# Transposes of small expert steps on 80 rows, and products that shift low parts upward on all 128 partitions

## The chip, the cores and the metric

The kernel runs on one core of a Trainium2 chip. The metric is the device time of one execution in microseconds (us). The kernel before took 1118.21 us, the median of 3 runs (1115.34 to 1118.33).

## The reference

One layer of a streaming encoder over 1024 tokens of width 1024, all in float32: a norm, one input projection, two mixers side by side (a spatial gating unit and a chunked linear recurrence), an output projection with a residual, and then a hierarchical mixture of experts with a residual and a last norm. The change touches the experts alone. Each token goes to one of 4 groups and to 2 of the 8 experts in that group:

```python
h = jax.nn.silu(xb @ w_gate[e]) * (xb @ w_up[e])
return h @ w_down[e]
```

`xb` holds the tokens of expert `e` (rows of 1024), `w_gate` and `w_up` are 1024x512 for each of the 32 experts, `w_down` is 512x1024. The results are weighted and added to the tokens' rows.

## The kernel before, in words

**Stages.** The mixers, the output projection and the router come first. From about 480 us on the kernel works through 32 expert steps; what follows is about those. The steps take the experts in the order of their number of tokens. The host code fixes a capacity for each place: 96 rows for the first three, then two places of 192 rows (a block of 128 and one of 64), and then single blocks of 128, 96, 80 and, for the 18 last, 64 rows. `KINDS` (line 51) mixes them: "s" is a small step of 64 rows, "L" a larger one of 80 to 128, "B" one of two blocks. So there are 20 blocks of 64 rows (18 of "s", and the second of each "B"), and nine times an "L" stands between small steps or after one, most often as s L s L.

**Precision.** Every float32 operand is taken apart into a high part (rounded to the matmul's format) and a low part (what is left), since TensorE reads the high format. Weights: `esplit` makes `ehi` on ScalarE (line 198) and `elo` on VectorE (line 199), a tile of 128x1024 at a time, from a raw tile `eraw` that a DMA brought. There are four buffers of `ehi` and of `elo`; raw tiles lie in a ring of 14 buffers of 1 MB, and at most four loads are in flight (`raw`, line 1030 on).

**Blocks over 64 rows** use three products for each piece of weights (`mm3`, lines 258 to 260): high by high, high by low, low by high, with the tokens as the stationary operand.

**Blocks of 64 rows** pack both parts of the tokens in one stationary operand of 128 columns: columns 0 to 63 the high part, 64 to 127 the low part (`split_rows`, `parts`, `block_mm`, lines 1059 and 1060). Two products do, and the sum stands in PSUM in two halves: partitions 0 to 63 hold the high part's, 64 to 127 the low part's. The halves have to be added. `low_out` (line 1096) copies partitions 64 to 127 from PSUM to a tile `low` on ScalarE (lines 1102, 1105); `low_in` (line 1108) then adds them into partitions 0 to 63 by a product of `low` with an identity `low_id` that stands on partitions 64 to 127 (line 1111): 64 contracted rows, 64 columns out, a moving operand of 512 columns. There is one such product for the gate sum and one for the up sum, and two for the down sum (`pair`, 1024 wide).

**Transposes.** The gathered tokens `xg` are turned by TensorE against `ident` (`xT`, line 1005: two groups of four transposes for a block), and so is the hidden activation `hh` (`hT_`, line 1022: one group of four). A transpose of a block of m rows contracts m rows and moves m columns. ScalarE and VectorE split what comes out into `x` and `h`. `hh` is written by a Silu on ScalarE (line 1119) and a multiplication on VectorE (line 1122), on m partitions.

**Order.** The code writes the order of every engine out by hand: `units` lists, quarter by quarter, the gate (G), up (U) and down (D) products of the steps, and `more` hangs the rest behind quarters. The low product of G stands behind the second quarter of U, and directly behind it the next step's first group of token transposes; the low product of U stands behind the second quarter of the D that follows. In most of the kernel D runs one step late.

Of the kernel before, what the change touches and what calls it, by code (L numbers as in the profile page):

```python
# [9 lines left out]
F32R = mybir.dt.float32r  # L10
BF16 = mybir.dt.bfloat16
I32 = mybir.dt.int32
AF = mybir.ActivationFunctionType
# [5 lines left out]
P = 128  # L19
# [33 lines left out]
HALF = 64  # L53
# [4 lines left out]
ORDER = (10, 0, 6, 7, 9, 1, 2, 3, 4, 5, 11, 12, 13, 8)  # L58
NXG = 5
AHEAD = 3  # L60
EPS = 1e-6


# [5 lines left out]
def body(ctx, tc, x, norm1_gain, w_in, v_gain, w_s, b_s, lower, out_gain, w_out, norm2_gain,  # L69
         w_gr, b_gr, w_er, b_er, w_gate, w_up, w_down, final_gain, out):  # L70
    nc = tc.nc
    V, A, T, G = nc.vector, nc.scalar, nc.tensor, nc.gpsimd
# [8 lines left out]
    def capacity(n):  # L81
        return STEP0 if n < FIXED else LEAST + MORE * sum(n < bound for bound in BOUNDS)
# [10 lines left out]
    def const(shape, dt, name):  # L93
        return consts.tile(shape, dt, name=name)

    ident = const([P, P], F32, "ident")
    V.memset(ident, 1.0)
    G.affine_select(ident, ident, pattern=[[1, P]], compare_op=OP.is_equal, fill=0.0, base=0, channel_multiplier=-1)

    low_id = const([P, HALF], F32R, "low_id")  # L100
    A.copy(low_id[HALF:], ident[HALF:, HALF:])
    before = const([P, P], BF16, "before")
    V.memset(before, 1.0)
    G.affine_select(before, before, pattern=[[1, P]], compare_op=OP.is_gt, fill=0.0, base=0, channel_multiplier=-1)
# [8 lines left out]
    eps = const([P, 1], F32, "eps")  # L113
    V.memset(eps, EPS)
    down8 = const([P, EPG], F32, "down8")
# [43 lines left out]
    def tp():  # L159
        return tpp.tile([P, 4, P], F32, name="tp", bufs=2)  # L160
# [34 lines left out]
    def split(hi, lo, raw, gain=None, sub=V):  # L195

        if gain is None:
            A.copy(hi, raw)  # L198
            sub.tensor_tensor(lo, raw, hi.bitcast(F32), op=OP.subtract)  # L199
        else:  # L200
            A.mul(hi, raw, gain)
            V.scalar_tensor_tensor(lo, raw, gain, hi.bitcast(F32), op0=OP.mult, op1=OP.subtract)  # L202
# [28 lines left out]
    def rstd(ss, n, pool, name, w):  # L231
        r = pool.tile([P, w], F32, name=name)
        A.activation(r, ss, AF.Sqrt, bias=eps, scale=1.0 / n)
        V.reciprocal(r, r)
        return r
# [13 lines left out]
    def norm_back(t):  # L249
        for half in range(2):  # L250
            pt = tp()
            for k in range(4):
                T.transpose(pt[:, k, :], n1s[t][:, (4 * half + k) * P:(4 * half + k + 1) * P], ident)
            hi = nh[:, 4 * half:4 * half + 4, t * P:(t + 1) * P]
            split(hi, nl[:, 4 * half:4 * half + 4, t * P:(t + 1) * P], pt)
# [17 lines left out]
    def proj_n(chunk, t, between=None):  # L273
        acc = bank("acc", 4)[:, :256]
        for k in range(KT):
            hi, lo = chunk["N"][k]
            ts = slice(P * t, P * t + P)
            mm3(acc, k, KT, nh[:, k, ts], nl[:, k, ts], hi, lo)
            if between and k == KT // 2 - 1:
                between()  # L280
        return acc
# [51 lines left out]
    for t in range(NT):  # L333
        if 1 < t < NT - 1:
            norm_back(t + 1)
        acc = proj_n(chunks[0], t, (lambda: norm_back(t + 1)) if t < 2 else None)
# [44 lines left out]
    while n < NE:  # L381
        c, o = capacity(n), n
# [150 lines left out]
    for p in range(2):  # L533
# [6 lines left out]
        for t in range(NT):  # L540
            acc = proj_n(chunk, t)
# [7 lines left out]
        r = rstd(ss, P, gp, "rsv", NT * 2)  # L549
# [7 lines left out]
        for half in range(2):  # L557
            for g in range(2):
# [4 lines left out]
                m = gp.tile([P, 4, P], F32, name="m", bufs=4)  # L563
# [7 lines left out]
        for g in range(2):  # L571
            gg = 2 * p + g
            accs = proj_t(chunk, g)
            if gg == H - 1:
# [3 lines left out]
                for k, (tag, n) in zip((4, 6, 0, 2), (("ht", 4), ("n2", 2), ("hT", 1), ("n2", 2))):  # L578
                    r = ra.tile([P, 2, 512], F32, name="woraw", tag=tag, bufs=n)
# [188 lines left out]
    def last_stats(half):  # L768

        t = NT - 1  # L770
        if half == 0:
# [3 lines left out]
            gained(t, 0)  # L775
            late[HOLD[0]] = V.tensor_scalar(rr[t][:, 0:1], rr[t][:, 0:1], 1.0 / D, EPS, op0=OP.mult, op1=OP.add)
            return
# [8 lines left out]
    def gained(t, half):  # L786
        cs = slice(512 * half, 512 * half + 512)
        G.tensor_tensor(n2s[t][:, cs], hts[t][:, cs], g2[:, cs], op=OP.mult)
# [23 lines left out]
    for k in (4, 6, 0, 2):  # L812
        r = wo1[k]
# [46 lines left out]
    low, high = range(4), range(4, KT)  # L860
# [45 lines left out]
    def open_pool(name, side="left"):  # L906
        return est.enter_context(tc.tile_pool(name=name, bufs=1, side=side, reuse_waits="tile"))
# [7 lines left out]
    es = open_pool("es")  # L915
# [48 lines left out]
        st["sl"].append((sl, m))  # L964

    fin = {}

    def next_xg():
        while any(xgs[nblk[0] % NXG] is v for v in fin.values()):
            nblk[0] += 1  # L970
        xg = xgs[nblk[0] % NXG]
        nblk[0] += 1
        return xg
# [12 lines left out]
    def split_rows(name, k, bufs, m):  # L986
        if m > HALF:
            return [ep.tile([P, k, P], F32R, name=name, bufs=bufs) for _ in range(2)]
        return [ep.tile([P, k, P], F32R, name=name, bufs=bufs)]

    def parts(tiles, ks, m):

        if m > HALF:
            return [t[:, ks, :m] for t in tiles]
        return [tiles[0][:, ks, c:c + m] for c in (0, HALF)]

    def xT(st, b, half, pts=None):

        (sl, m), xg = st["sl"][b], st["xg"][b]
        if half == 0:  # L1000
            st["x"].append(split_rows("x4", KT, 4, m))
        xv = xg.rearrange("p (c k) -> p k c", k=KT)
        pt = pts[half] if pts else tp()
        for k in range(0 if pts else 4):
            T.transpose(pt[:, k, :m], xv[:m, 4 * half + k, :], ident[:m, :m])  # L1005
        if half == 0 and st["plain"] == PLAIN0:

            st["xf"] = es.tile([P, 2 * 512], F32, name="xf0", tag="low")[:, :4 * m].rearrange("p (k c) -> p k c", k=4)
            V.tensor_copy(st["xf"], pt[:, :, :m])
        elif half == 1 and st["plain"] == PLAIN1:  # L1010
            st["xf"] = xfp.tile([P, 4, HALF], F32, name="xf")
            V.tensor_copy(st["xf"][:, :, :m], pt[:, :, :m])
            return
        split(*parts(st["x"][b], slice(4 * half, 4 * half + 4), m), pt[:, :, :m])

    def hT_(st, b):
        (sl, m), hh = st["sl"][b], st["h"][b]
        hv = hh.rearrange("p (c k) -> p k c", k=4)
        tiles = split_rows("h4", 4, 3, m)
        pt = tp()  # L1020
        for k in range(4):
            T.transpose(pt[:, k, :m], hv[:m, k, :], ident[:m, :m])
        split(*parts(tiles, slice(0, 4), m), pt[:, :, :m])
        st["hT"].append(tiles)

# [65 lines left out]
    def scatter(dst, sl, m, y, **how):  # L1091
        nc.gpsimd.indirect_dma_start(  # L1092
            out=dst[:, :], out_offset=bass.IndirectOffsetOnAxis(ap=sl[:m, 0:1], axis=0),
            in_=y[:m], in_offset=None, bounds_check=S - 1, oob_is_err=False, **how)

    def low_out(st, which):

        for acc, (sl, m) in zip(st["acc"][which], st["sl"]):
            if m <= HALF:
                low = es.tile([P, 2, 512], F32R, name="low", tag="low")  # L1100
                if which == 2:
                    A.copy(low[HALF:], st["pair"][HALF:])
                for c, a in enumerate(acc):
                    if which < 2:
                        A.copy(low[HALF:, c], a[HALF:])
                    st["low"].append((a[:m], low_id[HALF:, :m], low[HALF:, c]))

    def low_in(st):

# [4 lines left out]
    def post(st, which, last=False):  # L1114
        for b, (sl, m) in enumerate(st["sl"]):
            acc = st["acc"][which][b]
            if which == 0:
                st["h"].append(ep.tile([P, FE], F32, name="hh", bufs=2))
                A.activation(st["h"][b][:m], acc[0][:m], AF.Silu)
            elif which == 1:  # L1120
                hh = st["h"][b]
                V.scalar_tensor_tensor(hh[:m], acc[0][:m], sl.bitcast(F32)[:m, 2:3], hh[:m], op0=OP.mult, op1=OP.mult)
            else:
                y = yp.tile([P, D], F32, name="y", bufs=2)
                if b == len(st["sl"]) - 1:
                    A.copy(y[:m].rearrange("p (c n) -> p c n", c=2), st["pair"][:m])  # L1126
                else:
                    for c in range(2):
                        A.copy(y[:m, c * 512:(c + 1) * 512], acc[c][:m])
                st["y"].append(y)  # L1130
                if not last:
                    scatter(h_d, sl, m, y, compute_op=OP.add)
# [38 lines left out]
    def new_step(e, plain=()):  # L1171
        return dict(e=e, sl=[], xg=[], x=[], h=[], hT=[], y=[], low=[], acc={}, plain=plain)
# [121 lines left out]
    def prepare(s_):  # L1294

        while started[0] <= min(s_ + 1, NE - 1):
            start_step(started[0])
            started[0] += 1
        while listed_[0] <= min(s_ + 1, NE - 1):
            list_step(listed_[0])  # L1300
            listed_[0] += 1
        while gathered[0] <= min(s_, NE - 1):
            gather(sts[gathered[0]])
            gathered[0] += 1
# [80 lines left out]
    sts[0]["xg"].append(xgs[0])  # L1385
    prepare(AHEAD - 1)
    for half in range(2):
        xT(sts[0], 0, half, x0)
    i = 0
    for u in units:  # L1390
# [14 lines left out]
        else:  # L1405
# [3 lines left out]
            if which == 0 and q == 0:  # L1409
                prepare(s_ + AHEAD)  # L1410
                if NE // 2 <= s_ < NE // 2 + 5:
# [5 lines left out]
    st = sts[last]  # L1417
# [10 lines left out]
    with tc.For_i(0, n_ov, 1) as j:  # L1428
# [3 lines left out]
        st = new_step(e)  # L1432
# [45 lines left out]
```

## Time and profile before

| | |
|---|---|
| median of 3 runs | 1118.21 us |
| profiled execution, whole | 1115.45 us |
| its span, first to last instruction | 1113.5 us |
| share of the span: TensorE (PE), VectorE (DVE), ScalarE (ACT), GpSimd (POOL) | 95%, 73%, 68%, 17% |
| DMA, mean over the span | 238 GB/s |

PE is busy nearly all the time, but its records overlap: a product's record lasts from its start until its result has left the array, so what a product costs in a row of products is the distance from its start to the next start. The prediction reads PE by such distances.

### The profile page before, as it was taken

What the parts mean: (1) busy time and instruction counts of PE and PEld (TensorE: products, weight loads), DVE (VectorE), ACT (ScalarE), POOL (GpSimd) and SP (SyncE); (2) the same over time, 40 slices, a digit from 0 to 9 for tenths busy, and PEclk for the clock granted to TensorE, in tenths of its full rate; (3) what the DMA queues carried; (4) which work ended last, traced back from release to release, by engine and by line L of the source; (5) the groups of instructions that cost most, each with busy time, mean ns of one, the idle gap of its engine ahead of it and who ended that gap; (6) DMA issues with size and microseconds to landing.
All of it is one profiled execution on the core that took longest, in us unless ns stands there. A gap on an engine that the chain in (4) does not pass through costs nothing.

```text
span 1113.5 us, 16412 instructions
## 1 busy us (share of the span) xinstructions
PE 1061.1 (95%) x5602; PEld 816.0 (73%) x5602; DVE 809.9 (73%) x1438; ACT 758.4 (68%) x1058; POOL 188.8 (17%) x203
## 2 busy tenths in 40 slices
PE   7999999999999999998999999999999999999962
PEld 7978989899898898776667667667666666666531
DVE  6576665664544555757996799998879999999773
ACT  7665564654323432546887898998889889998783
POOL 3000000000002121543112222312213212121022
PEclk9999999999999999868999999999999999999986
DMA  8211111111115351599998999999999999999943
GB/s 272 87 39 39 39 39 39 38 39 33 45 39 178 106 215 46 213 401 340 380 393 315 325 373 377 400 366 368 361 322 384 382 371 388 381 386 394 353 145 100
DMA packets 67797, 264.75 MB, mean 238 GB/s; under 512 B 9990, under 2 KB 32574, under 8 KB 42112
## 3 DMA queue, kind: packets, MB, share of 16 engines
q1 hardware_dynamic: 54896, 230.72, 55.0%
q0 software_dynamic: 12528, 31.92, 10.3%
q8 instruction: 45, 0.74, 0.3%
q10 hardware_dynamic: 288, 1.05, 0.2%
q14 instruction: 40, 0.33, 0.1%
HBM read 244.60 MB, written 24.81 MB: 242 GB/s over the span
## 4 chain that ended last, share of the span: by engine, by line
PE 26%; DMA 11%; ACT 9%; DVE 4%; issue 3%; POOL 0%; POOLq 0%; ACTq 0%; SPq 0%; DVEq 0%
ACT ehi L198 5%; DMA eraw<-in_w_down_dram 5%; PE acc L258 4%; PE acc L259 3%; PE acc L260 3%; DMA eraw<-in_w_up_dram 3%; DVE elo L199 3%; PE acc L1060 2%; DMA eraw<-in_w_gate_dram 2%; PE acc L1059 2%; PE tp L1005 2%; PE pair L258 1%; PE pair L259 1%; PE pair L260 1%; PE pair L1060 1%
## 5 line engine op out<-in xcount | busy, mean ns | idle before, releaser
L199 DVE TENSOR_TENSOR elo<-eraw,ehi 128x1024 fp32r<-128x1024 f32 x374 | 442.6, 1218 | 64.1 <-ACT ehi L198 61.5
L198 ACT CAST ehi<-eraw 128x1024 fp32r<-128x1024 f32 x374 | 379.8, 1050 | 30.5 <-PE acc L260 8.8
L1060 PE MATMUL acc<-elo,x 128*128 128x512 f32 x304 | 124.5, 410 | 9.3 <-DVE elo L199 8.8
L1092 POOL DMA_INDIRECT h_d<-y,sl x34 | 57.5, 1693 | 425.6 <-ACT y L1126 367.4
L1059 PE MATMUL acc<-ehi,x 128*128 128x512 f32 x304 | 125.6, 413 | 2.5 <-ACT ehi L198 2.4
L258 PE MATMUL acc<-whiN,nh 128*128 128x256 f32 x384 | 109.0, 284 | 1.8 <-ACT nh L198 1.8
L260 PE MATMUL acc<-whiN,nl 128*128 128x256 f32 x384 | 108.3, 282 | 0.6 <-DVE nl L199 0.6
L259 PE MATMUL acc<-wloN,nh 128*128 128x256 f32 x384 | 108.4, 282 | 0.1
L258 PE MATMUL acc<-ehi,x 128*96 128x512 f32 (+2 forms) x220 | 89.6, 407 | 0.0
L259 PE MATMUL acc<-elo,x 128*96 128x512 f32 (+2 forms) x220 | 87.1, 396 | 0.0
L260 PE MATMUL acc<-ehi,x 128*96 128x512 f32 (+2 forms) x220 | 86.7, 394 | 0.0
L1060 PEld LDWEIGHTS acc<-elo,x 128*128 128x128 f32 x304 | 57.4, 189 | 33.9 <-DVE elo L199 23.4
L259 PE MATMUL acc<-nl,whiT 128*128 128x512 f32 x192 | 77.7, 405 | 0.0
L258 PE MATMUL acc<-nh,whiT 128*128 128x512 f32 x192 | 77.5, 404 | 0.0
L260 PE MATMUL acc<-nh,wloT 128*128 128x512 f32 x192 | 77.0, 401 | 0.0
L258 PEld LDWEIGHTS acc<-whiN,nh 128*128 128x128 f32 x384 | 72.4, 188 | 2.2 <-ACT nh L198 2.1
L260 PEld LDWEIGHTS acc<-whiN,nl 128*128 128x128 f32 x384 | 72.3, 188 | 0.8 <-DVE nl L199 0.8
L1059 PEld LDWEIGHTS acc<-ehi,x 128*128 128x128 f32 x304 | 58.1, 191 | 20.0 <-issue 6.2
L259 PEld LDWEIGHTS acc<-wloN,nh 128*128 128x128 f32 x384 | 72.3, 188 | 0.5 <-DVE wloN L202 0.3
L1059 PE MATMUL pair<-ehi,h 128*128 128x512 f32 x160 | 67.5, 422 | 0.9 <-DVE h L199 0.9
L1060 PE MATMUL pair<-elo,h 128*128 128x512 f32 x160 | 65.1, 407 | 0.9 <-DVE elo L199 0.7
L580 POOL DMA_DIRECT2D woraw<-in_w_out_dram x4 | 2.8, 717 | 325.1 <-PE acc L260 325.1
(382 smaller groups left out, 2182.1 us busy)
## 6 DMA issues: line engine op xcount, KB each, us to landing
eraw<-in_w_gate_dram SPq DMA_DIRECT2D x64, 1024.0 KB, 10.3
eraw<-in_w_up_dram SPq DMA_DIRECT2D x64, 1024.0 KB, 11.2
eraw<-in_w_down_dram SPq DMA_DIRECT2D x64, 1024.0 KB, 10.6
wraw<-in_w_in_dram SPq DMA_DIRECT2D x96, 128.0 KB, 2.4
ht<-in_x_dram SPq DMA_DIRECT2D x8, 512.0 KB, 3.8
eraw<-h_d SPq DMA_DIRECT2D x4, 1024.0 KB, 7.8
out_dram<-eraw SPq DMA_DIRECT2D x4, 1024.0 KB, 4.2
h_d<-ht POOLq DMA_DIRECT2D x7, 512.0 KB, 3.2
```

Of the source, the lines that this page charges most:

```text
L198: A.copy(hi, raw)
L199: sub.tensor_tensor(lo, raw, hi.bitcast(F32), op=OP.subtract)
L258: T.matmul(acc, lh, rh, start=k == 0, stop=False)
L259: T.matmul(acc, lh, rl, start=False, stop=False)
L260: T.matmul(acc, ll, rh, start=False, stop=k == n - 1)
L580: nc.gpsimd.dma_start(r, w_out2[k * P:(k + 2) * P, 512:1024].rearrange("(k p) c -> p k c", p=P))
L1005: T.transpose(pt[:, k, :m], xv[:m, 4 * half + k, :], ident[:m, :m])
L1059: T.matmul(acc, tiles[0][:, k], hi, start=k == 0, stop=False)
L1060: T.matmul(acc, tiles[0][:, k], lo, start=False, stop=k == n - 1)
L1092: nc.gpsimd.indirect_dma_start(out=dst[:, :], out_offset=bass.IndirectOffsetOnAxis(ap=sl[:m, 0:1], axis=0), in_=y[:m], in_offset=None, bou ...
```

## The change

Transposes of a block of fewer than 80 rows take 80 rows and 80 columns (`WIDE`), so that 64-row blocks read 16 rows more of `xg` and `hh` than they use; the Silu on ScalarE writes 80 partitions so that those rows of `hh` hold numbers. `low` becomes one tile for the whole stage whose lower 64 partitions are set to zero once; `low_id` becomes 128 partitions by 96 columns, zero outside the old identity. The low product contracts all 128 partitions and writes 96, and adds zeros to 64 to 95.

```diff
+WIDE = 80
...
-    low_id = const([P, HALF], F32R, "low_id")
-    A.copy(low_id[HALF:], ident[HALF:, HALF:])
+    low_id = const([P, 96], F32R, "low_id")
+    A.mul(low_id, ident[:, :96], 0.0)
+    A.copy(low_id[HALF:, :HALF], ident[HALF:, HALF:])
...
+    lows = []
...
+        r = max(m, WIDE)
         for k in range(0 if pts else 4):
-            T.transpose(pt[:, k, :m], xv[:m, 4 * half + k, :], ident[:m, :m])
+            T.transpose(pt[:, k, :r], xv[:r, 4 * half + k, :], ident[:r, :r])
...
+        r = max(m, WIDE)
         for k in range(4):
-            T.transpose(pt[:, k, :m], hv[:m, k, :], ident[:m, :m])
+            T.transpose(pt[:, k, :r], hv[:r, k, :], ident[:r, :r])
...
             if m <= HALF:
-                low = es.tile([P, 2, 512], F32R, name="low", tag="low")
+                if not lows:
+                    lows.append(es.tile([P, 2, 512], F32R, name="low", tag="low"))
+                    A.mul(lows[0][:HALF], ident[:HALF, None, 0:1].to_broadcast([HALF, 2, 512]), 0.0)
+                low = lows[0]
                 if which == 2:
                     A.copy(low[HALF:], st["pair"][HALF:])
                 for c, a in enumerate(acc):
                     if which < 2:
                         A.copy(low[HALF:, c], a[HALF:])
-                    st["low"].append((a[:m], low_id[HALF:, :m], low[HALF:, c]))
+                    st["low"].append((a[:96], low_id, low[:, c]))
...
             if which == 0:
                 st["h"].append(ep.tile([P, FE], F32, name="hh", bufs=2))
-                A.activation(st["h"][b][:m], acc[0][:m], AF.Silu)
+                r = max(m, WIDE)
+                A.activation(st["h"][b][:r], acc[0][:r], AF.Silu)
```

No engine's instructions change places. Two are added, both on ScalarE. One stands at the start of the program (the zeros of `low_id`), the other in the fourth step, ahead of the first copy of low parts. ScalarE there, before (line 198 is the high part of a weight tile, 1105 the copy of low parts, 1119 the Silu):

```order
L198 CAST ehi<-eraw_5820 128x1024
L1105 CAST low<-acc_6155 64x512
L198 CAST ehi<-eraw_5820 128x1024
L198 CAST ehi<-eraw_5866 128x1024
L1119 ACTIVATE hh<-acc_6155 64x512
```

And in the changed kernel (201, 1114 and 1129 are the same lines there, 1108 is new):

```order
L201 CAST ehi<-eraw_5821 128x1024
L1108 ACTIVATE low<-ident 64x1024
L1114 CAST low<-acc_6156 64x512
L201 CAST ehi<-eraw_5821 128x1024
L201 CAST ehi<-eraw_5867 128x1024
L1129 ACTIVATE hh<-acc_6156 80x512
```

The zero fill stands between a weight tile's high part and the copy of low parts; the Silu's form is 80 partitions instead of 64, and all else is where it was.

## Rows read from the trace of the kernel before

**Rows 1.** The page's first part: busy time, share of span, instructions.

```profile
PE 1061.1 (95%) x5602; PEld 816.0 (73%) x5602; DVE 809.9 (73%) x1438; ACT 758.4 (68%) x1058; POOL 188.8 (17%) x203
```

**Rows 2.** One s-L period: busy PE, PEld, DVE, ACT, POOL; clock, DMA share, GB/s.

```profile
891.70:926.14 34.44, 34.15 (x149) 22.49 (x148) 31.73 (x33) 30.80 (x38) 7.25 (x7) 1.00 1.02 380
```

**Rows 3.** Chain that ended last, 857 to 930: start us, us, what.

```profile
913.80 0.59 PE tp L1005 x4
...
923.97 1.24 DVE elo L199
...
925.25 0.50 PE acc L1060
```

**Rows 4.** Groups by line and shape, PE: count, busy us, mean ns.

```profile
L1005 PE MATMUL tp<-ident,xg 64*128 64x64 f32 x160 | 26.1, 283 | 0.2
...
L1111 PE MATMUL acc<-low,low_id 64*64 64x512 f32 x40 | 17.6, 441 | 1.6 <-ACT low L1105 1.6
...
L1111 PE MATMUL pair<-low,low_id 64*64 64x512 f32 x40 | 13.9, 428 | 1.1 <-ACT low L1102 1.1
L1022 PE MATMUL tp<-ident,hh 64*128 64x64 f32 x80 | 13.9, 295 | 2.3 <-DVE hh L1122 2.3
```

**Rows 5.** PE in order, transposes of 64 rows: start us, us, what.

```profile
909.89 0.39 PE L260 MATMUL acc<-ehi,x 128*80 128x512 f32 x1
910.21 0.65 PE L1005 MATMUL tp<-ident,xg 64*128 64x64 f32 x4
910.79 0.46 PE L258 MATMUL acc<-ehi,x 128*80 128x512 f32 x1
911.09 0.39 PE L259 MATMUL acc<-elo,x 128*80 128x512 f32 x1
```

**Rows 6.** PE in order, transposes of 80 rows.

```profile
894.02 0.40 PE L1059 MATMUL acc<-ehi,x 128*128 128x512 f32 x1
894.26 0.40 PE L1060 MATMUL acc<-elo,x 128*128 128x512 f32 x1
894.50 0.56 PE L1005 MATMUL tp<-ident,xg 80*128 80x80 f32 x4
894.86 0.44 PE L258 MATMUL pair<-ehi,h 128*80 128x512 f32 x1
895.14 0.40 PE L259 MATMUL pair<-elo,h 128*80 128x512 f32 x1
```

**Rows 7.** PE in order, a low product by itself.

```profile
897.46 0.40 PE L260 MATMUL pair<-ehi,h 128*80 128x512 f32 x1
897.78 0.45 PE L1111 MATMUL acc<-low,low_id 64*64 64x512 f32 x1
898.16 0.46 PE L258 MATMUL pair<-ehi,h 128*80 128x512 f32 x1
898.46 0.40 PE L259 MATMUL pair<-elo,h 128*80 128x512 f32 x1
```

**Rows 8.** PE in order, a low product ahead of transposes of 64 rows.

```profile
594.31 0.45 PE L1111 MATMUL acc<-low,low_id 64*64 64x512 f32 x1
594.32 0.65 PE L1005 MATMUL tp<-ident,xg 64*128 64x64 f32 x4
594.90 0.51 PE L258 MATMUL acc<-ehi,x 128*128 128x512 f32 x1
595.24 0.39 PE L259 MATMUL acc<-elo,x 128*128 128x512 f32 x1
```

**Rows 9.** ACT in order, in the period's L part; idle before, releaser.

```profile
914.42 0.37 ACT L198 CAST x<-tp 128x256 fp32r<-128x256 f32 x1 [0.92 <-PE tp L1005]
```

**Rows 10.** DVE in order, the same stretch.

```profile
906.41 4.82 DVE L199 TENSOR_TENSOR elo<-eraw,ehi 128x1024 fp32r<-128x1024 f32 x4 [0.61 <-ACT ehi L198]
```

**Rows 11.** Groups by line and shape, ACT.

```profile
L1102 ACT CAST low<-pair 64x1024 fp32r<-64x1024 f32 x20 | 20.2, 1010 | 5.1 <-PE pair L1060 4.7
```

**Rows 12.** DMA issues: count, KB each, median us from issue to landing.

```profile
eraw<-in_w_up_dram SPq DMA_DIRECT2D x64, 1024.0 KB, 11.2
```

## The prediction

> **What bounds the kernel now.** I read the page's busy shares first. PE stands at 95% of the span [rows 1], but its records overlap, so that proves nothing yet. The second view is busy time by stretch, over one period of a small and a larger step in the expert stage. It takes 34.44 us, with PE busy 34.15, DVE 31.73, ACT 30.80, a full clock, and DMA at 380 GB/s [rows 2]. So PE is ahead of the two engines that split weights, but by 8 to 11% only. The third view is the chain that ended last. In this period it lies on PE up to the transposes at 913.80, then on ACT and DVE until the split at 923.97 is done, and then on PE again from 925.25 [rows 3]. That is the picture to keep: the larger step, with three products for each piece of weights, is paced by PE; the small step, with two, is paced by the splits. What PE saves in the first part counts, what it saves in the second is waited away.
>
> The fourth view is PE in order of time. In a plain row one product starts 0.24 us after the other (894.02, 894.26), and a group of transposes of 80 rows starts 0.24 us after the product before it, is followed after 0.36 us, and the second product after it starts 0.28 us later [rows 6]: 0.88 us. The same group on 64 rows is entered after 0.32 us, followed after 0.58, and left after 0.30 [rows 5]: 1.20 us. So the 64-row form costs 0.32 us more, though it moves fewer columns and the records of single transposes hardly differ. A low product shows the same: 0.32, 0.38 and 0.30 us [rows 7], 1.00 where three plain products take 0.24 each, 0.72, so 0.28 too much. I read both as a price for each visit to the 64-row form: a pause before, one after, and weight loads that don't run ahead.
>
> The Trainium skill says the same from the other end: in "TensorEngine Tiling (Array Packing)", section Tiling Modes, changing the tiling mode, unlike changing the tile, drains the engine. The rows agree with about 0.1 us at the entry. The same page's section Performance Considerations speaks against this change: contracted dimensions up to 64 are to be tiled by rows, since two tiles then work in parallel. By that rule small products should stay on 64 rows.
>
> Here is what the rows say on that. Where a low product (partitions 64 to 127) stands directly before transposes of 64 rows (partitions 0 to 63), they start 0.01 us apart, and both together take 0.59 us [rows 8], against 0.58 for the transposes alone [rows 5]. There the low product is free, and the change takes that away: 0.24 us for the product and 0.36 for the transposes make 0.60. Body for body that is no gain, only the pauses go (0.32 to 0.24 before, 0.34 to 0.28 after, so 0.1 us).
>
> **The change part by part.**
>
> *Counting the visits.* 160 transposes of tokens on 64 rows are 40 groups of four; 80 of the activation are 20 groups; 40 single low products; 40 low products in pairs, so 20 pairs [rows 4]. Together 120 groups. By the order of the code 10 single low products stand right before a 64-row group of token transposes (8 of G before a small step's first group, 2 of U before the last group of a "B" step's second block), and one, at the very end, before transposes of the activation. Those 11 are the combined visits. The other 98 each stand alone, also the 11 low products ahead of larger transposes. Worth: 98 visits by 0.30 us (between 0.28 and 0.32) are 29.4, and 11 by 0.1 are 1.1: 30.5 us of PE time.
>
> *What a period gets.* It has six plain visits: the low product of G, that of U, the activation's group, two groups of tokens, and the pair. Five lie in the part that PE paces; the pair lies after 914, where ACT and DVE pace. So 5 by 0.30 is 1.5 us. ACT waits there 0.92 us for one group of transposes [rows 9], DVE 0.61 us for ACT at one place [rows 10]. These idle times are the room into which PE's gain can go. DVE has 34.44 - 31.73 = 2.7 us idle in the whole period; after a gain of 1.5 it would be busy 96% of it. So DVE becomes late in places, first at the splits behind the last token transposes. I take 1.3 of the 1.5. Bounds: 0.5, if DVE catches most, and 1.8, if the pair's visit counts as well. Nine periods: 11.7 us.
>
> *The rest of the expert stage.* 98 - 54 = 44 plain visits and the 11 combined ones are in the first steps, around the two "B" steps and in the last three: 13.2 + 1.1 = 14.3 us. Two small steps in a row are paced by splits, a "B" by PE. I take 55%, 8 us; bounds 4 and 14.
>
> *Wider forms.* The changed transposes move 80 columns like those of [rows 6], so their price is known. The new low product (128 rows, 96 columns out, 512 moved) has no row of its own; the nearest are plain products of the same 512 columns, with 0.24 us between starts. Below that it can't go, as it moves as many columns; above I keep 0.38, today's distance [rows 7]. I take 0.24. The Silu writes 80 partitions instead of 64, with the same columns: nothing.
>
> *Added.* The zero fill of `low` on ACT, 64x1024, is like the copy of 64x1024 on line 1102: 1.0 us [rows 11], once, between splits in the fourth step. ACT's queue holds the copy of low parts and the next splits behind it, and PE needs both. I charge 1.0 us (bounds 0 and 1.0). The zeros of `low_id` come at the program's start, while the first input is loaded: nothing, at most 0.3 us if that cover is gone. `low` is now one tile; it had one buffer already, so each copy waits for the same products as before.
>
> *Sum* against the profiled execution: 1115.45 - 11.7 - 8 + 1.0 = 1096.8 us. It lies 2.8 us under the median of the runs shown, so on the median's scale I forecast 1099.5 us, rounded to 1099.
>
> **The rivals.**
>
> *Splits take over (20%).* DVE at 31.73 and ACT at 30.80 of 34.44 us are near their end, and PE at 925.25 already waits for a split. If they catch most of it: nine by 0.5 and 4 elsewhere, less 1.0, so 7.5 us: 1110.7. For it: DVE starts splits only when ACT is done, so it never gets to 100%. Against: the waits that I would fill [rows 9, 10] are waits for PE.
>
> *Everything on PE counts (7%).* 30.5 - 1.0: 1088.7. Against: the chain leaves PE in every period.
>
> *The loads take over (4%).* Four loads in flight that land after 11.2 us [rows 12] are one in 2.8 us; a period needs twelve, one in 2.87 now and 2.76 after a gain of 1.3. So DMA is as fast as asked for now and a little slow afterwards. Against: 14 buffers by 2.87 are 40 us, less 11 for landing, so a full ring holds some 29 us of lead, more than all that is to be gained. Were the lead gone, periods would stay at 34.44 and only 8 - 1 remain: 1111.
>
> *The pauses aren't the form's (5%), the slower side.* One mechanism: they belong to a change of operand, the low product keeps its 0.38 and its pauses on 128 rows, and transposes stay at 1.20; then the ten free low products turn into 0.38 us each, 3.8, and the fill adds 1.0: 1123. It decides if transposes of 80 rows behind a plain product are entered after 0.32 us; [rows 6] has 0.24 for them. The skill's advice on row tiling, named above, would end on this side too. Also here: the gain is eaten to nothing, within 0.3% (4%).
>
> **How the numbers follow.** Forecast 60%, own range 1092 to 1106. With the rivals on both sides the range 1089 to 1112 leaves under 2 in 10 out: the slower case, part of the gain-to-nothing case, and the far end of full gain. 0.3% is 3.4 us, about what a measurement of this kernel can tell from no change. Faster by more: forecast 60, splits 19, all on PE 7, loads 3: 0.89. Within: 0.07. Slower: 0.04.
>
> **What would show it.** In the changed profile no PE product of the expert stage has 64 contracted rows in the line of the low products, and transposes are 80 wide. The distances around them should be 0.24, 0.36 and 0.28 us, and around low products 0.24. A period of a small and a larger step should be near 33.1 us with DVE still 31.7 busy; PE should wait more for `elo` after small steps. ACT's wait for transposes, 0.92 us now, should shrink. One ACT row of about 1 us should appear in the fourth step. I am wrong if the period stays at 34.4 though the distances shrink (splits or loads took it), or if the distances don't shrink (the form was not the cause).

## The result, and the profile after

The changed kernel takes 1098.72 us, the median of 4 runs (1097.68 to 1100.03), against 1117.00 us (4 runs, 1115.34 to 1118.33) before. The ratio is 0.9837, with a 95% interval of 0.9824 to 0.9851: 18.3 us faster. The forecast was 1099.

The profiled execution took 1097.68 us with a span of 1095.7 (before: 1115.45 and 1113.5), so 17.8 us less span. Against the forecast for it, 1096.8, that is 0.9 us more. The median came 0.8 us under the 1099.5 of the sum, since the changed kernel's median lies 1.0 us over its profiled execution and not 2.8 us. The page's first part, with the columns of [rows 1]:

```profile
PE 1035.5 (95%) x5602; PEld 820.9 (75%) x5602; DVE 805.1 (73%) x1438; ACT 757.7 (69%) x1060; POOL 224.9 (21%) x203
```

PE has as many instructions as before and 25.6 us less busy time at the same share; ACT has two instructions more. The share alone says nothing of the gain.

Busy time over the same s-L period as in [rows 2], from the low product of G to the same place one period later:

```profile
881.84:914.88 33.04, 32.40 (x149) 22.54 (x148) 31.28 (x33) 30.65 (x38) 8.41 (x7) 1.00 1.02 381
```

The period is 1.40 us shorter (34.44 to 33.04). DVE is now busy 95% of it, ACT 93%, PE 98%; the granted clock is 1.00, the higher of its two levels, as before.

The groups by line and shape, PE, with the columns of [rows 4] (lines 1010, 1028 and 1120 are 1005, 1022 and 1111 of before):

```profile
L1010 PE MATMUL tp<-ident,xg 80*128 80x80 f32 x200 | 28.5, 264 | 0.1
...
L1120 PE MATMUL acc<-low,low_id 128*96 128x512 f32 x40 | 16.0, 401 | 1.0 <-ACT low L1114 1.0
...
L1028 PE MATMUL tp<-ident,hh 80*128 80x80 f32 x100 | 15.3, 275 | 2.3 <-DVE hh L1132 2.3
...
L1120 PE MATMUL pair<-low,low_id 128*96 128x512 f32 x40 | 13.0, 407 | 1.1 <-ACT low L1111 1.1
```

The 160 transposes of 64 rows have joined the 40 of 80 rows, and the mean record fell from 283 to 264 ns. By these means the change looks like almost nothing. Its price stands in the distances between starts. PE in order of time (start us, us, what), the transposes of a small step's tokens, to be read against [rows 5]:

```profile
899.24 0.40 PE L263 MATMUL acc<-ehi,x 128*80 128x512 f32 x1
899.47 0.56 PE L1010 MATMUL tp<-ident,xg 80*128 80x80 f32 x4
899.83 0.44 PE L261 MATMUL acc<-ehi,x 128*80 128x512 f32 x1
900.11 0.39 PE L262 MATMUL acc<-elo,x 128*80 128x512 f32 x1
```

0.23, 0.36 and 0.28 us where 0.32, 0.58 and 0.30 stood: 0.87 instead of 1.20. A low product by itself, in the same view, against [rows 7]:

```profile
887.48 0.40 PE L263 MATMUL pair<-ehi,h 128*80 128x512 f32 x1
887.72 0.40 PE L1120 MATMUL acc<-low,low_id 128*96 128x512 f32 x1
887.95 0.39 PE L261 MATMUL pair<-ehi,h 128*80 128x512 f32 x1
888.18 0.39 PE L262 MATMUL pair<-elo,h 128*80 128x512 f32 x1
```

0.24, 0.23, 0.23 where 0.32, 0.38 and 0.30 stood: the low product costs what a plain product costs.

What makes the difference stands in the weight loads (PEld in order: start us, us, what, idle time before and releaser). Here are the loads of the low product and of the product behind it, before and after:

```profile
897.78 0.13 PEld L1111 LDWEIGHTS acc<-low,low_id 64*64 64x64 f32 x1 [0.40 <-issue]
898.15 0.15 PEld L258 LDWEIGHTS pair<-ehi,h 128*80 128x80 f32 x1 [0.25 <-issue]
...
887.49 0.16 PEld L1120 LDWEIGHTS acc<-low,low_id 128*96 128x96 f32 x1
887.72 0.15 PEld L261 LDWEIGHTS pair<-ehi,h 128*80 128x80 f32 x1
```

Before, both loads start together with their own products (897.78 and 898.16 in [rows 7]), and the loads stand idle for 0.40 and 0.25 us ahead of them, with nothing in the profile that they waited for ("issue"). After, each starts beside the product ahead (887.48 and 887.72), as in a row of plain products. That is the pause that the prediction read: around the 64-row form no load ran ahead. It was so for all 40 single low products and all 40 groups of token transposes on 64 rows before; in the changed kernel these loads start 0.23 us ahead on the median.

The combined place, against [rows 8]:

```profile
594.12 0.40 PE L1066 MATMUL acc<-elo,x 128*128 128x512 f32 x1
594.35 0.40 PE L1120 MATMUL acc<-low,low_id 128*96 128x512 f32 x1
594.59 0.56 PE L1010 MATMUL tp<-ident,xg 80*128 80x80 f32 x4
594.95 0.48 PE L261 MATMUL acc<-ehi,x 128*128 128x512 f32 x1
595.26 0.39 PE L262 MATMUL acc<-elo,x 128*128 128x512 f32 x1
```

Both no longer start together (0.24 us apart), and take 0.60 together, as worked out before. With the pauses around them the place is 0.1 us shorter: 1.14 us from the first to the last of these rows, where it was 1.26 (from 593.98, the row below, to the last row of [rows 8]).

```profile
593.98 0.40 PE L1060 MATMUL acc<-elo,x 128*128 128x512 f32 x1
```

The zero fill, ACT in order of time, is one row of 1.06 us in the fourth step:

```profile
552.36 1.06 ACT L1108 ACTIVATE low<-ident 64x1024 fp32r<-64x1024 f32 x1
```

The chain that ended last, within the period (columns of [rows 3]):

```profile
902.82 0.42 PE tp L1010 x4
...
912.81 1.24 DVE elo L202
...
915.04 0.24 PE acc L1120
```

It has the shape of [rows 3]: PE up to the second group of token transposes, then the splits to the end of the small step, then PE. In [rows 3] 11.4 us lie from the transposes' start to the last split's end; here 11.2. The small step's half hardly got shorter. From the period's start to these transposes it was 22.1 us (891.70 to 913.80) and is 21.0 (881.84 to 902.82): 1.1 of the 1.40 us came out of the half that PE paces. ACT's waits there, for that group of transposes, shrank as said: 0.92 us in [rows 9], 0.74 here.

```profile
903.26 0.37 ACT L201 CAST x<-tp 128x256 fp32r<-128x256 f32 x1 [0.74 <-PE tp L1010]
```

**Where the 17.8 us of span come from**, by the start of ACT's first weight split of each step in the two traces. That of the second step came 1.0 us later than before (510.3 against 509.3; what lies ahead of it scatters by more, from 506.2 to 513.4 in the runs below). Nine s-L periods, each from the low product of G to the same place one period later, gave 11.9 us. The zero fill cost 1.0. The rest of the expert stage gave 7.9: 11.9 + 7.9 - 1.0 - 1.0 = 17.8. The nine are not alike: seven gave 1.3 to 1.5 us each, and the two that follow two small steps in a row gave 1.2 and 0.7.

### The profile page after: what moved, and what is told of

Read it like the earlier page. It is cut to its first block, busy times and chain, and to the rows that moved or that the text cites. A ratio compares the mean times of both kernels' runs of the same rounds, so it can differ in the third digit from the quotient of the medians.

```text
span 1095.7 us, 16412 instructions
## 1 busy us (share of the span) xinstructions
PE 1035.5 (95%) x5602; PEld 820.9 (75%) x5602; DVE 805.1 (73%) x1438; ACT 757.7 (69%) x1060; POOL 224.9 (21%) x203
## 4 chain that ended last, share of the span: by engine, by line
PE 26%; ACT 10%; DMA 8%; DVE 5%; issue 4%; POOL 0%; POOLq 0%; ACTq 0%; SPq 0%; DVEq 0%
ACT ehi L201 6%; PE acc L262 4%; DVE elo L202 4%; PE acc L263 4%; PE acc L261 4%; DMA eraw<-in_w_down_dram 3%; DMA eraw<-in_w_gate_dram 3%; PE acc L1066 3%; DMA eraw<-in_w_up_dram 2%; PE acc L1065 2%; PE tp L1010 1%; PE pair L262 1%; PE pair L263 1%; PE pair L261 1%; PE pair L1066 1%
## 5 line engine op out<-in xcount | busy, mean ns | idle before, releaser
L1098 POOL DMA_INDIRECT h_d<-y,sl x34 | 93.0, 2736 | 374.3 <-ACT y L1136 305.5
L1066 PE MATMUL acc<-elo,x 128*128 128x512 f32 x304 | 127.5, 419 | 14.4 <-DVE elo L202 13.1
```

What stands on the lines that cost most here:

```text
L1066: T.matmul(acc, tiles[0][:, k], lo, start=False, stop=k == n - 1)
L1098: nc.gpsimd.indirect_dma_start(out=dst[:, :], out_offset=bass.IndirectOffsetOnAxis(ap=sl[:m, 0:1], axis=0), in_=y[:m], in_offset=None, bou ...
```

## The experiments

The edits are shown against the changed kernel unless said. Medians of before are those of the same chip, 1116 to 1117 us. "Period" is the s-L period above.

### One half of the change at a time

**Transposes alone.** The low products go back to 64 contracted rows, and the zero fill goes.

```diff
-                if not lows:
-                    lows.append(es.tile([P, 2, 512], F32R, name="low", tag="low"))
-                    A.mul(lows[0][:HALF], ident[:HALF, None, 0:1].to_broadcast([HALF, 2, 512]), 0.0)
-                low = lows[0]
+                low = es.tile([P, 2, 512], F32R, name="low", tag="low")
...
-                    st["low"].append((a[:96], low_id, low[:, c]))
+                    st["low"].append((a[:m], low_id[HALF:, :m], low[HALF:, c]))
```

> Transposes and Silu on 80 rows, low products as before. My theory (each visit to the 64-row form costs 0.30 us, and it counts where PE paces): 49 plain visits go, 14.7 us of PE time; the ten low products that ran beside 64-row transposes now stand alone, 0.2 us more each, so 12.6 us net. Of a small-larger period three visits in PE's part go: 34.44 becomes 33.6 to 33.7 us. Total about 9.5 us less than before: 1107 to 1108. Rival (the pauses belong to the low products alone): distances around the transposes stay, total unchanged. Rival (a microsecond of PE counts the same everywhere, 0.6 as in the whole change): 7.6 us less, about 1109.

1106.82 us (1102.16 to 1108.00, 6 runs), 10.1 under before; ratio 0.9908 (0.9890 to 0.9925). Busy time by stretch, one period:

```profile
882.74:916.29 33.55, 33.19 (x150) 22.29 (x149) 31.40 (x33) 30.84 (x38) 7.27 (x7) 1.00 1.02 383
```

0.89 us less: three visits by 0.3, the two groups of token transposes and the activation's. Both numbers came a little better than expected, by 0.05 us in the period and 0.2 in the total. The rival that put 7.6 us on everything lies below the interval of the gain (8.4 to 12.3).

**Low products alone.** Both kinds of transposes and the Silu go back to 64.

```diff
-            T.transpose(pt[:, k, :r], xv[:r, 4 * half + k, :], ident[:r, :r])
+            T.transpose(pt[:, k, :m], xv[:m, 4 * half + k, :], ident[:m, :m])
...
-            T.transpose(pt[:, k, :r], hv[:r, k, :], ident[:r, :r])
+            T.transpose(pt[:, k, :m], hv[:m, k, :], ident[:m, :m])
```

> Low products on 128 rows and 96 columns with the zero fill, transposes on 64 rows. My theory: 49 plain visits go (18 of U, 11 of G before larger transposes, 20 pairs), 14.2 us of PE time, less ten places where the low product was free beside 64-row transposes, 0.2 us more each. In a period two of the three visits lie in PE's part: 34.44 becomes 33.9 us. Total 6 to 7 us less: about 1110. Rival (PE counts the same everywhere): 7.3 us less and the period 33.9 as well, so the total alone does not tell these apart; e3 and e4 do. Rival (the change of operand makes the pause): distances around low products stay at 0.32 and 0.30.

1109.84 us (1108.98 to 1112.92, 6 runs), 7.1 under before; ratio 0.9937 (0.9918 to 0.9957). Period and total came as expected. The two halves add up to 10.1 + 7.1 = 17.2 of 18.3, within their intervals. The period is 33.93, 0.51 less, where its two single low products paced by PE promise 0.56. PE in order, a combined place:

```profile
595.66 0.40 PE L1066 MATMUL acc<-elo,x 128*128 128x512 f32 x1
595.89 0.40 PE L1120 MATMUL acc<-low,low_id 128*96 128x512 f32 x1
596.22 0.65 PE L1010 MATMUL tp<-ident,xg 64*128 64x64 f32 x4
596.80 0.51 PE L261 MATMUL acc<-ehi,x 128*128 128x512 f32 x1
597.14 0.39 PE L262 MATMUL acc<-elo,x 128*128 128x512 f32 x1
```

The low product no longer starts with the transposes but 0.33 us ahead of them, and they keep their 0.58 and 0.34. From the first of these rows to the last it is 1.48 us, where it was 1.26 before. So widening the low product alone costs about 0.2 us at each of these places, where it had been free.

**The activation's transposes alone.** The low products as in the first experiment, the token transposes as in the second.

> Only the activation's transposes and the Silu take 80 rows: 20 visits, 6 us of PE time. In a period the one of the small step lies in PE's part. My theory: the period goes from 34.44 to 34.15 to 34.2 us, total 4 us less. Rival (a microsecond of PE counts the same everywhere): 34.26 and 3.6 us.

1108.95 us (1108.03 to 1110.67, 6 runs), 7.9 under before; ratio 0.9925 (0.9908 to 0.9942). The profiled execution has 5.9 us less in the expert stage. Its period:

```profile
889.56:923.62 34.06, 33.75 (x150) 22.42 (x149) 31.68 (x33) 30.82 (x38) 7.28 (x7) 1.00 1.02 388
```

0.38 us less, for one visit worth 0.3. Both numbers of the expectation were too small; the visit counts in full and a little more. The nine periods make 3.5 of these 5.9 us; the rest lies outside them. Why the runs gained 2 us more than the profiled execution, the slowest of the six, is open; the stages ahead scatter by as much.

**Only the pair's low products.** Everything on 64 rows but the products of the down sum, which take 128; the zero fill stays.

```diff
-                    st["low"].append((a[:96], low_id, low[:, c]))
+                    st["low"].append((a[:96], low_id, low[:, c]) if which == 2 else (a[:m], low_id[HALF:, :m], low[HALF:, c]))
```

> Only the pairs of low products of the down sums take 128 rows and 96 columns, with the zero fill: 20 visits, 6 us of PE time, as many as with the activation alone. In a period the pair lies in the part that the splits pace. My theory: the period stays at 34.40 to 34.44 us; the total is 0 to 2 us less. Rival (a microsecond of PE counts the same everywhere): period 34.26, total 3.6 us less.

1115.00 us (1111.61 to 1116.59, 12 runs), 1.9 under before; ratio 0.9976 (0.9963 to 0.9988). The period:

```profile
891.29:925.69 34.40, 33.80 (x150) 22.60 (x149) 31.74 (x33) 30.82 (x38) 7.26 (x7) 1.00 1.01 377
```

34.40, against 34.44: PE is busy 0.35 us less and the period takes just as long. The same pause is saved as in the third experiment (the pair's starts are 0.23, 0.47 and 0.23 us apart from 920.09 on, where they were 0.32, 0.61 and 0.34 from 920.56 on), but in the small step's half, and it is waited away: 0.04 us for this visit, 0.38 for the activation's. So a visit counts by where it lies. The half isn't paced by splits everywhere to the same degree: in the last five of the nine periods the pair gave 0.05 us or less, in the first four 0.14 to 0.40. The kernel holds the zero fill too, which shows by itself here: the first split of the fifth step, seen from that of the second, is 1.0 us later than before. In the experiment with the low products alone the weight splits of the fourth step are 1.0 us ahead of before up to the fill and 0.05 ahead right behind it; in the changed kernel they fall back by 0.96 us at the same place.

### What it is in the form that costs

**128 rows in, 64 columns out; 64 rows in, 96 columns out; transposes of 65 rows.** Three kernels with one run each.

```diff
-                    st["low"].append((a[:96], low_id, low[:, c]))
+                    st["low"].append((a[:m], low_id[:, :m], low[:, c]))          # first
+                    st["low"].append((a[:96], low_id[HALF:], low[HALF:, c]))     # second
...
-WIDE = 80
+WIDE = 65                                                                        # third
```

> The changed kernel, but low products with 128 contracted rows and 64 columns out instead of 96. If only the contracted rows make the pauses: 0.23 or 0.24 us between starts around single low products, as in the changed kernel. If a product that fills only half of the columns costs the same drain: 0.32 before, 0.30 or more after.

> The changed kernel, but low products with 64 contracted rows (partitions 64 to 127) and 96 columns out. If the contracted rows make the pauses: 0.32 before, 0.37 for the product and 0.30 after, as in the kernel before. If it was the columns: 0.24 throughout. The ten low products ahead of small transposes no longer run beside them, since those take 80 rows: 0.32, 0.37 and then transposes.

> The changed kernel with transposes of small blocks on 65 rows and columns instead of 80. If what counts is that a product contracts more than 64 rows: entered after 0.24 us, 0.35 to 0.36 for the four, left after 0.28 to 0.32, and the period stays at 33.04 us. If the price falls gradually with the rows: between those and the 0.32, 0.58 and 0.30 of 64 rows.

1101.81, 1103.39 and 1100.61 us; periods of 33.06, 33.60 and 33.04. PE in order around a low product with 128 rows in and 64 columns out:

```profile
889.33 0.39 PE L263 MATMUL pair<-ehi,h 128*80 128x512 f32 x1
889.55 0.40 PE L1120 MATMUL acc<-low,low_id 128*64 128x512 f32 x1
889.79 0.39 PE L261 MATMUL pair<-ehi,h 128*80 128x512 f32 x1
890.02 0.40 PE L262 MATMUL pair<-elo,h 128*80 128x512 f32 x1
```

Around one with 64 rows in and 96 columns out:

```profile
889.55 0.40 PE L263 MATMUL pair<-ehi,h 128*80 128x512 f32 x1
889.88 0.47 PE L1120 MATMUL acc<-low,low_id 64*96 64x512 f32 x1
890.27 0.46 PE L261 MATMUL pair<-ehi,h 128*80 128x512 f32 x1
890.57 0.40 PE L262 MATMUL pair<-elo,h 128*80 128x512 f32 x1
```

Around transposes of 65 rows:

```profile
900.09 0.40 PE L263 MATMUL acc<-ehi,x 128*80 128x512 f32 x1
900.32 0.55 PE L1010 MATMUL tp<-ident,xg 65*128 65x65 f32 x4
900.68 0.43 PE L261 MATMUL acc<-ehi,x 128*80 128x512 f32 x1
900.96 0.39 PE L262 MATMUL acc<-elo,x 128*80 128x512 f32 x1
```

Distances of 0.22, 0.24 and 0.23 in the first, 0.33, 0.39 and 0.30 in the second, 0.23, 0.36 and 0.28 in the third. So the columns out cost nothing, and the contracted rows make the pause. In the transposes one row over 64 takes all of it away; there one moved column goes along with the row, but the low products, with 512 moved columns in both forms, have the same pause. By visits and period the 96 columns of the changed kernel are not needed; 64 would do. The two theories of a gradual price and of a price per operand fall with it. The totals of the first and the third say nothing against this, though they lie above all four runs of the changed kernel: in both traces the granted clock from 780 to 800 us was 0.91 on the mean, in part at the half of its two levels (1.00 in the changed kernel, with PE busy 17.9 to 18.0 us in all three), and they lost 1.4 to 1.5 us in the step that lies there; 2.2 to 2.3 us more went behind the first weight split of the last step. Why the end took longer is open.

### How much room is left

**Shorter weight splits, on the kernel before and on the changed one.** Each split of weights takes 768 of its 1024 columns, and the products read within these; the outputs are not the reference's. The edit is the same in both kernels.

```diff
-        split(hi, lo, r[:, 1024 * c:1024 * c + 1024], sub=sub)
+        raw = r[:, 1024 * c:1024 * c + 1024]
+        A.copy(hi[:, :768], raw[:, :768])
+        sub.tensor_tensor(lo[:, :768], raw[:, :768], hi[:, :768].bitcast(F32), op=OP.subtract)
...
-                    fs = slice(k * FE, (k + 1) * FE)
+                    fs = slice(k * 256, k * 256 + FE)
...
-                    cs = slice(c * 512, c * 512 + 512)
+                    cs = slice(c * 256, c * 256 + 512)
```

> The kernel before with splits of expert weights cut to 768 of 1024 columns on ACT and DVE; the products read columns 0 to 511 and 256 to 767, so that their number and size stay (the outputs then are not the reference's). With the splits a quarter shorter PE should pace everything. My theory: a small-larger period is then PE's own, 34.44 less the waits of 0.3 to 0.6, so 33.8 to 34.1 us; total 5 to 12 us less than before.

> The changed kernel with the same shortened splits. My theory: nothing is waited away now, so the period is shorter than that of e10 by all six visits, 1.8 to 2.0 us instead of 1.4, near 32.0; the total is 24 to 30 us under that of e10. Rival (the loads are the next bound, with a lead of 12 us left in the changed kernel): the last periods stay at 33 us or more and the difference is 18 to 22 us.

On the kernel before: 1099.50 us (1096.94 to 1100.43), 16.7 under before, ratio 0.9844 (0.9826 to 0.9862). One period:

```profile
879.84:913.26 33.42, 33.42 (x150) 22.67 (x149) 26.04 (x32) 26.08 (x38) 6.16 (x7) 1.00 1.02 377
```

PE is busy in every moment of it, and the period is 1.02 us shorter than in [rows 2], where only 0.29 us were shown as idle. The expected 5 to 12 us were too little: overlapping records hide two thirds of PE's waits. The starts show them. In the small step's half of [rows 2], away from the visits, six distances are 0.31 to 0.67 us where a plain one is 0.23 (the longest from 924.58 to 925.25, of which the records show 0.27 as idle), together 1.1 us too long. The two periods behind two small steps in a row gained 2.4 and 1.6 us by shorter splits, the seven others 1.0 to 1.1: where the change itself gained least, the splits hold PE back most.

On the changed kernel: 1092.66 us (1087.95 to 1096.14), ratio to before 0.9776 (0.9751 to 0.9801), 6.8 under the same splits on the kernel before. The expected difference of a period came, as shown below, but neither total did, and the trace, that of the slowest of the four runs, says why. One period before 840 us and one after it:

```profile
692.93:724.41 31.48, 31.47 (x149) 23.95 (x148) 26.08 (x33) 26.04 (x38) 7.79 (x7) 1.00 1.02 379
...
862.93:899.25 36.32, 33.46 (x149) 22.49 (x148) 26.11 (x33) 26.05 (x38) 6.84 (x6) 1.00 1.01 377
```

With no engine but PE in the way the period is 31.48, 1.94 under 33.42: all six visits by 0.32, as expected (the same period of the other kernel takes 33.43). At 859 us it was 16.7 us ahead of the other kernel. Then the loads had no lead left. ACT's waits from 860 to 1020 us (engine, line, what it waited for: us in all, times, longest; line 1059 is the weight split there):

```profile
ACT ehi L1059 <- DMA eraw<-in_w_gate_dram: 21.1, 15, 2.2
...
ACT ehi L1059 <- DMA eraw<-in_w_down_dram: 8.9, 10, 3.8
```

No such wait stands in the trace of the changed kernel between 540 and 1020 us. But there too the lead shrinks. By an estimate from the DMA records, with the loads taken to land in their order, a tile lay ready up to 39 us before its split at first and 10 to 12 us at the least, near the end (before: from 41 to about 20). The same estimate gives 3 to 4 us where the shortened splits already wait, so it is some 3 us too high. So the loads are what comes next, when 7 to 9 us more are saved in this stage.

**The same units in other orders.** Since the small step's half is paced by splits and the other by PE, I mixed them. Once as G of a step, D of the one before, U; then by quarters (U0 U1 D0 U2 D1 U3 D2 D3, steps 2 to 30, and the same up to step 28). The first two lines below are the edit of the one, the rest that of the others; the lines that hang transposes and additions behind other quarters to suit are left out.

```diff
-        order_ += [f"G{s_}", f"U{s_}"] + ([f"D{s_ - 1}"] if s_ > 1 else [])
+        order_ += [f"G{s_}"] + ([f"D{s_ - 1}"] if s_ > 1 else []) + [f"U{s_}"]
...
-    for i, v in enumerate(order_):
-        for q in range(4):
+    ...
+        if order_[i][0] == "U" and 2 <= int(order_[i][1:]) < NE - 1:
+            seq += [(i, 0), (i, 1), (i + 1, 0), (i, 2), (i + 1, 1), (i, 3), (i + 1, 2), (i + 1, 3)]
```

> The changed kernel with the order of units G, D of the step before, U instead of G, U, D: stretches paced by PE and by the splits then alternate after 4 weight tiles instead of 12, and the 4 buffers of splits can level them. My theory (the two paces alternate, and the rest of PE's gain is lost to that): the period falls from 33.04 us to 32.2 to 32.6, and the total by 4 to 8 us below the changed kernel, to about 1092. Rival (the loads or the sum of the waits of the split engines hold it): the period stays within 0.2 us. Slower is possible if the activation's transposes, now one unit ahead of their use instead of two, come late.

> The changed kernel with the quarters of U and of the D of the step before mixed (U0 U1 D0 U2 D1 U3 D2 D3), the activation's transposes three quarters behind the multiplication as before. In e9 PE waited some 2 us a step for that multiplication, which stands behind three splits in DVE's queue; here that should be gone. My theory: stretches paced by PE and by splits alternate within the 4 buffers, the period falls from 33.04 to 32.2 to 32.7 us and the total to 1092 to 1096. Rival (the sum of waits between ACT and DVE holds it): no change within 0.2 us a period. Slower if the transposes or their splits come late again.

> As e12, but the last three steps keep the order of the changed kernel. In e12 the stretches before step 29 began 3.6 us earlier than in the changed kernel, nearly all of it gained around runs of small steps and the two-block steps, and the last steps gave 2.2 us back. My theory: that loss comes from mixing near the end; without it the total is 3 to 4 us under the changed kernel's 1098.72, so about 1095. Rival: the loss is a lead of loads that is used up sooner, and comes all the same: 1097 to 1098.

G, D, U: 1154.99 us (1151.66 to 1156.41), ratio to before 1.0334 (1.0319 to 1.0348). It was slower for the reason that the expectation held open. PE in order, with idle time before and releaser, two steps in a row:

```profile
935.75 0.71 PE L1028 MATMUL tp<-ident,hh 80*128 80x80 f32 x4 [1.66 <-DVE hh L1132]
...
953.36 0.68 PE L1028 MATMUL tp<-ident,hh 80*128 80x80 f32 x4 [2.05 <-DVE hh L1132]
```

The multiplication that makes `hh` stands behind three weight splits in DVE's queue. From 540 to 1060 us PE waits for it 24 times, 48.2 us in all, and the granted clock is 0.95 there (1.00 in the changed kernel from 540 to 1040). The changed kernel is 56.3 us faster.

By quarters: 1097.81 us (1096.69 to 1099.43), ratio to before 0.9840 (0.9825 to 0.9855), so not to be told from the changed kernel. The period is still 33.04, as the rival had it. By the first splits of the steps it is 3.6 us ahead of the changed kernel at the 30th of the 32, gained where small and two-block steps follow one another, 2.9 ahead at the last step, and 0.5 behind at the end of the span. Up to step 28 only: 1095.98 us (1095.19 to 1097.64), ratio 0.9819 (0.9805 to 0.9832), 20.0 under before; the intervals overlap with the changed kernel's, so it is no proven gain either. Its expectation put the loss on the mixing near the end, but its own lead of 2.6 us at the last step is gone at the end of the span too, without any mixing there, so that isn't shown.

## Why the prediction was right, step by step

- **A price per visit, 0.28 to 0.32 us.** Right, and shown: the distances came out as 0.23, 0.36 and 0.28 around transposes, 0.24, 0.23, 0.23 around low products, and 31.48 against 33.42 gives 0.32 for each of six visits. The weight loads show the mechanism: none ran ahead around the 64-row form.
- **The low product at 0.24 us**, between bounds of 0.24 and 0.38. Right; the nearest row, a plain product of the same 512 columns, was the one to go by.
- **The combined visits.** Right: 0.60 together, and with the pauses 0.1 us less than before. What they hid shows when only one of the two forms is widened (0.2 us more at each of ten places).
- **1.3 of 1.5 us in a period.** 1.40 came in this period, so a little low. Five of six visits were taken to count; the pair's alone gave 0.04, the activation's alone 0.38, all three of transposes 0.89, the low products 0.51.
- **Nine periods, 11.7.** 11.9 came. That is closer than the working deserves: it took all nine to be alike, and the two with 1.2 and 0.7 us make up for the seven with 1.3 to 1.5.
- **The rest of the expert stage, 8.** 7.9 came, 55% of 14.3. The 55% was a guess within bounds of 4 and 14, so that it fits so well is luck; no run takes this part by itself.
- **The sum.** 11.7 + 8 - 1.0 = 18.7 against 11.9 + 7.9 - 1.0 = 18.8 from the second step on. The 0.9 us between 1096.8 and the profiled 1097.68 lie ahead of it, where the traces differ by 1.0.
- **The zero fill, 1.0.** Right, by the splits of the fourth step in three kernels (0.95 to 0.96 us). The Silu on 80 partitions costs nothing, as taken: 0.59 us each in both traces.
- **The places that would show it.** DVE was expected at 31.7 us of the new period and had 31.28. PE's wait for `elo` grew from 0.3 to 0.6 us a period, which is small.
- **Splits take over (20%).** Not at this gain. But the splits, with DVE at 31.28 and ACT at 30.65 of 33.04 us, keep back the pair's visit and some 0.2 us more: with shorter splits the same change gives 1.94 a period instead of 1.40.
- **The loads take over (4%).** Not reached here, but closer than the prediction had it. It took the ring's 29 us as a lead that lasts; the loads are slower than the demand in both kernels, and by the estimate above 7 to 9 us were left at the end. It is what stopped the changed kernel with shortened splits.
- **The pauses aren't the form's (5%).** Fallen: the boundary lies between 64 and 65 contracted rows for the transposes, and somewhere between 64 and 128 for the low products.

The rule that contracted dimensions up to 64 are better tiled by rows ("TensorEngine Tiling (Array Packing)" of the Trainium skill, section Performance Considerations) does not hold here, if the 64-row form is read as row tiling, as the prediction did (no row names the mode). Where small products stand singly between full ones, the padded form won. Where two of them meet on different halves they do run side by side ([rows 8], 0.01 us apart), but with its pauses even that place was 0.1 us longer than the padded form. Longer runs of small products on both halves were not tried.

## What to carry to other kernels

Price an operation on PE by the distance from start to start, with its neighbours' on both sides, not by its record: the mean record of a transpose differed by 19 ns, its visit by 0.32 us a group of four. A small product that stands alone among full ones is better padded beyond 64 contracted rows with zeros, as long as the moved columns stay the same or grow little (64 to 80 in the transposes). And such savings count only in the stretches that PE paces: find these by the chain first, then multiply, and see how much lead the loads have left before asking for more.

## What the runs showed of the hardware

- The pause has an edge, not a slope: 64 contracted rows cost it, 65 and 80 (transposes) and 128 (low products) do not, whatever the columns out (128 rows with 64 columns out: 0.22 to 0.24 us; 64 rows with 96: 0.33, 0.39, 0.30).
- Around a product of 64 contracted rows the weight loads don't run ahead: they stand idle 0.40 us before its load and 0.25 us before the next product's.
- Leaving a group of transposes costs 0.05 us even on 80 rows (0.28 against 0.23 between plain products); this is left in the changed kernel.
- PE's records hide its waits: 0.29 us idle in a period before, 1.02 us gained when the other engines were relieved. What the end of a PE record marks, no run here shows; the distances are taken from starts alone.
- DMA moved 377 to 388 GB/s in all periods shown here, most of it in 1 MB loads of weights, four in flight, and was busy all the time (a share of 1.01 or 1.02); at 31.48 us a period the loads could not follow.
